# One-hot rows of the gate products, laid out with the places innermost, on one Trainium2 core

## The chip, the cores and the metric

The kernel runs on one core of a Trainium2 chip. That core has four compute engines that each take their own instructions in order: TensorE (PE in the rows; its weight loads are a row kind of their own, PEld), VectorE (DVE), ScalarE (ACT) and GpSimd (POOL), beside SyncE (SP), which here only starts transfers. The metric is the device time of one execution in microseconds (us); of several executions the median is taken.

## The reference, cut to what matters

One layer of a decoder trunk over 1024 prompt tokens and 32 sample tokens: a projection, three token mixers, an output projection, and then a product-key mixture of 16384 single-row experts (PEER). For every token, eight heads choose 16 experts each, so 128 pairs of an expert number and a gate. With `i = 128 a + b` as the expert number, the layer's last part is

```
act  = gelu(x @ peer_u[i])                 # 128 chosen experts of each token
out  = sum over the 128 of  gate * act * peer_v[i]
```

The kernel treats four of the nine token tiles (tiles 2 to 5, 512 tokens, called dense here) without gathering: it computes the scores of all 16384 experts and needs, for each token, a 128 x 128 table of gates `G[a, b]`, which is zero but for the chosen experts. The change is in the code that builds this table.

## The kernel before, in words

**The table of gates.** `g_weights(i, t)` builds it for one dense tile of 128 tokens. Two transposes put the tile's 128 expert numbers and gates on the partitions (partition = place in the list of 128 choices, column = token). From the numbers come `a` and `b` as 16-bit floats in the tile `fx`, and the gate as a 16-bit head and a 16-bit rest. Then, for blocks of `BB = 16` tokens, VectorE writes the tile `ab`, which holds three one-hot arrays: the one for `a` (`ab[:, 0]`), the one for `b` times the head of the gate (`ab[:, 1]`), and the one for `b` times the rest (`ab[:, 2]`, also called `eq`). ScalarE does the last multiplication for the first `NL = 6` tokens of a block. TensorE multiplies, for each token, the transposed `a` rows by the two `b` arrays (two 128 x 128 matmuls into the tile `pgm`, four tokens to a bank). ScalarE copies each bank out to two tiles `gs`, and for each 32 tokens two transfers of 1 MB write these to the DRAM table `G_d`. There are 4 tiles x 8 blocks = 32 blocks and 1024 such matmuls. `ab` has two buffers, each `gs` half has one.

**What runs beside it.** A tile's table can start when the tile is routed (`g_route`, `g_choice`: matmuls `pqr` and top-k work on VectorE). `g_pre` computes the scores of 32 of the 128 expert blocks ahead (matmuls `psd`, line 1070). The other five tiles are done by gathering: POOL starts one indirect transfer for each expert row of 128 tokens (`row`, line 1272); VectorE uses a `peer_u` row (line 1299), TensorE a pair of `peer_v` rows (`acc`, line 1356); six buffers hold such rows. All of these share the engines in one program order. When the last table is written the kernel closes its front tiles and goes on to the dense part (`psd` and `po` matmuls), which lasts to the end.

**The order of the work** is set by generators with declared costs and by a scheduler that orders each engine's instructions by a modelled timeline.

Of the kernel before, what the change touches and what calls it, by code (L numbers as in the profile page):

```python
# [8 lines left out]
F16 = mybir.dt.float16  # L9
# [4 lines left out]
AF = mybir.ActivationFunctionType  # L14
ALU = mybir.AluOpType
AX = mybir.AxisListType

P = 128
# [36 lines left out]
BB = 16  # L55
NL = 6
PRE = [4 * g + 3 for g in range(32)]
GROUP = 4
SW, SU, SV, SG_, SC = 2.0 ** 8, 2.0 ** 8, 2.0 ** 6, 2.0 ** 12, 0.25
# [18 lines left out]
def kernel(ctx: ExitStack, tc: tile.TileContext, A, O):  # L78
    nc = tc.nc
    mm, tr = nc.tensor.matmul, nc.tensor.transpose  # L80
    V, S = nc.vector, nc.scalar
# [72 lines left out]
    def bank(name, shape=(P, 512)):  # L154
        return psum.tile(list(shape), F32, name=name, tag="f", bufs=5)

    def keep(name, shape, dtype=F32, bufs=1):
        return small.tile(list(shape), dtype, name=name, tag=name, bufs=bufs)
# [123 lines left out]
    C = {}  # L282
# [707 lines left out]
    scale = keep("scale", [P, 4])  # L990
# [28 lines left out]
    def g_weights(i, t):  # L1019

        sc = cur["build"]
        if "rep" not in C:
            C["rep"] = sc.tile("rep", [P, P, BB], F16)
            V.tensor_copy(C["rep"], iota16.unsqueeze(2).to_broadcast([P, P, BB]))
        IF, G = (top[t][2][:, e].rearrange("p h j -> p (h j)") for e in range(2))
        pt = bank("ptg", (P, 2, P))
        tr(pt[:, 0, :], IF, ident)
        tr(pt[:, 1, :], G, ident)
        ix = sc.tile("ix", [P, 2, P], I32)
        V.tensor_copy(ix[:, 0, :], pt[:, 0, :])  # L1030
        V.tensor_scalar(ix[:, 1, :], ix[:, 0, :], P - 1, None, op0=ALU.bitwise_and)
        V.tensor_scalar(ix[:, 0, :], ix[:, 0, :], 7, None, op0=ALU.arith_shift_right)
        fx = sc.tile("fx", [P, 4, P], F16, 2)
        fl = sc.tile("fl", [P, P], F32, 2)
        V.tensor_copy(fx[:, 0:2, :], ix)
        V.tensor_scalar(fx[:, 2, :], pt[:, 1, :], SG_, None, op0=ALU.mult)
        V.scalar_tensor_tensor(out=fx[:, 3, :], in0=pt[:, 1, :], scalar=SG_, in1=fx[:, 2, :], op0=ALU.mult,
                               op1=ALU.subtract)
        V.tensor_copy(fl, fx[:, 3, :])
        yield 0.4, 1.0, 0  # L1040
        for b in range(P // BB):
            ab = sc.tile("ab", [P, 3, P, BB], F16, 2)
            f = [fx[:, j, b * BB:b * BB + BB].unsqueeze(1).to_broadcast([P, P, BB]) for j in range(4)]
            eq = ab[:, 2]
            V.tensor_tensor(out=ab[:, 0], in0=C["rep"], in1=f[0], op=ALU.is_equal)
            V.tensor_tensor(out=eq, in0=C["rep"], in1=f[1], op=ALU.is_equal)
            V.tensor_tensor(out=ab[:, 1], in0=eq, in1=f[2], op=ALU.mult)  # L1047
            V.tensor_tensor(out=eq[:, :, NL:], in0=eq[:, :, NL:], in1=f[3][:, :, NL:], op=ALU.mult)
            for j in range(NL):
                S.activation(eq[:, :, j], eq[:, :, j], AF.Copy, scale=fl[:, b * BB + j:b * BB + j + 1])  # L1050
            if b * BB % TB == 0:
                gs = [sc.tile("gs", [P, 64, TB], F32, 2) for _ in range(2)]
            for t4 in range(0, BB, 4):
                pg = bank("pgm", (P, 4, P))
                for j in range(4):
                    for e in range(2):
                        mm(pg[:, j, :], lhsT=ab[:, 0, :, t4 + j], rhs=ab[:, 1 + e, :, t4 + j], start=(e == 0), stop=(e == 1))  # L1057
                t0 = b * BB % TB + t4
                for e in range(2):
                    S.activation(gs[e][:, :, t0:t0 + 4].rearrange("p c t -> p t c"), pg[:, :, 64 * e:64 * e + 64], AF.Copy)  # L1060
                yield 0.6, 1.1, 0.4 * MB
            if (b + 1) * BB % TB == 0:
                for e in range(2):
                    nc.sync.dma_start(G_d[i * (P // TB) + b * BB // TB, :, 64 * e:64 * e + 64, :], gs[e])
# [197 lines left out]
    iota16 = keep("iota16", [P, P], F16)  # L1262
# [264 lines left out]
    def g_gates():  # L1527
        yield from wait("build")
        for i, t in enumerate(DENSE):
            yield from wait(("routed", t))  # L1530
            yield from g_weights(i, t)
            ready.add(("weights", t))
# [208 lines left out]
```

## Time and profile before

| | |
|---|---|
| median of three runs | 3297.21 us (3287.35 to 3303.12) |
| the profiled execution, own time | 3293.14 us |
| its span, first to last instruction | 3291.4 us |
| TensorE busy / VectorE / ScalarE / GpSimd, share of the span | 87% / 67% / 31% / 40% |
| mean transfer rate | 297 GB/s |

The busy share of TensorE is an average over stages with other limits. The tables are built from about 1080 us to 1710 us of the span; what happens there is read from that stretch.

### The profile page before, as it was taken

To read this page: it belongs to the slowest core of one execution; us is meant where nothing else is said; L and a number is where in the kernel's file an instruction comes from. 1 tells how busy PE (TensorE), PEld (TensorE's weight loads), DVE (VectorE), ACT (ScalarE), POOL (GpSimd) and SP (SyncE) were. 2 spreads that over 40 slices of the span, in tenths; PEclk is the share of its full clock that TensorE was granted. 3 is DMA by queue.
4 is the path that set the end of the run, shared out by engine and by line. 5 is a ranking of instruction groups with operands and counts; after the bars stand their busy time and mean duration, and the time that the engine had idled before them with its cause. 6 is when DMAs were issued, how large, how long until landed. Compare 5 with 4: busy or idle time off the path is not lost.

```text
span 3291.4 us, 45024 instructions
## 1 busy us (share of the span) xinstructions
PE 2878.7 (87%) x16366; PEld 1477.0 (45%) x16366; DVE 2206.4 (67%) x5761; ACT 1019.0 (31%) x1654; POOL 1323.3 (40%) x1096
## 2 busy tenths in 40 slices
PE   6878993587976899997788699999999999999996
PEld 3447942334654566444342464433444443333331
DVE  2443998777788877655445678766777776555546
ACT  3413243111021444456561124232323322222220
POOL 0000366545444533432233410544555554455544
PEclk8988996688978899996559799999999999999997
DMA  8743898889898888777578864999999999999986
GB/s 296 249 172 134 293 350 297 294 308 325 317 345 304 298 292 302 261 286 274 206 257 310 311 209 156 343 331 328 364 354 356 352 354 346 344 353 354 351 314 208
DMA packets 376498, 979.03 MB, mean 297 GB/s; under 512 B 37477, under 2 KB 116452, under 8 KB 372172
## 3 DMA queue, kind: packets, MB, share of 16 engines
q0 software_dynamic: 156672, 570.49, 47.8%
q1 hardware_dynamic: 219604, 405.67, 35.5%
q8 instruction: 128, 2.10, 0.3%
q14 instruction: 94, 0.77, 0.1%
HBM read 907.07 MB, written 69.02 MB: 297 GB/s over the span
## 4 chain that ended last, share of the span: by engine, by line
PE 57%; DMA 11%; DVE 6%; issue 4%; ACT 2%; POOL 1%; SPq 0%; POOLq 0%; DVEq 0%; ACTq 0%
PE psd L1070 17%; PE po L1177 16%; PE acc L1356 7%; PE pgm L1057 6%; DMA row<-in_peer_v,iT 6%; PE pqr L880 5%; DMA row<-in_peer_u,ii 3%; PE py L809 2%; POOL row L1272 1%; DVE row L1299 1%; ACT ab L1050 1%; DMA wo<-in_w_o 1%; PE ps L890 1%; DMA e<-x_d 1%; PE pvp L279 1%
## 5 line engine op out<-in xcount | busy, mean ns | idle before, releaser
L1272 POOL DMA_INDIRECT row<-in_peer_u,ii x544 | 672.4, 1236 | 1036.4 <-DVE ii L1295 316.0
L1272 POOL DMA_INDIRECT row<-in_peer_v,iT x544 | 647.6, 1190 | 875.0 <-PE acc L1356 494.8
L1299 DVE SCALAR_TENSOR_TENSOR row<-row,x2u 128x1024 f32<-128x1024 f32 x544 | 660.2, 1217 | 304.0 <-DMA row<-in_peer_u,ii 288.1
L1070 PE MATMUL psd<-xd,us 128*128 128x512 f16 x3072 | 709.5, 381 | 18.7 <-DMA xd<-xd_d 8.3
L1177 PE MATMUL po<-vs,coef 128*128 128x512 f16 x3072 | 701.3, 379 | 3.0 <-ACT coef L1167 1.7
L1070 PEld LDWEIGHTS <-us 128*128 128x128 f16 x3072 | 295.8, 99 | 430.9 <-issue 79.8
L1177 PEld LDWEIGHTS <-coef 128*128 128x128 f16 x3072 | 291.0, 98 | 430.3 <-issue 89.0
L1356 PE MATMUL acc<-row,cexp 128*32 128x512 f32 x2176 | 330.7, 662 | 127.4 <-DMA row<-in_peer_v,iT 127.1
L1057 PE MATMUL pgm<-ab 128*128 128x128 f16 x1024 | 265.4, 419 | 43.6 <-DVE ab L1047 23.1
L880 PE MATMUL pqr<-x2T,wpq 128*128 128x128 f32 (+1 forms) x2304 | 286.0, 283 | 1.9 <-DVE ns_s L707 0.7
L880 PEld LDWEIGHTS pqr<-x2T,wpq 128*128 128x128 f32 x2304 | 280.9, 199 | 10.9 <-DVE CT_s L712 1.5
L1160 ACT ACTIVATE act<-psd,scale 128x512 f32<-128x512 f32 x96 | 65.8, 685 | 513.5 <-PE psd L1070 503.7
L1057 PEld LDWEIGHTS <-ab 128*128 128x128 f16 x1024 | 149.7, 148 | 154.0 <-issue 40.4
L1186 DVE SCALAR_TENSOR_TENSOR acc<-po,scale,acc 128x512 f32<-128x512 f32 x248 | 182.9, 744 | 45.7 <-PE po L1177 40.4
L1162 DVE SCALAR_TENSOR_TENSOR act<-act,scale,g 128x512 f32<-128x512 f32 x128 | 95.7, 748 | 151.6 <-ACT act L1160 128.1
L1140 ACT ACTIVATE vs<-v 128x1024 f16<-128x1024 f32 x128 | 135.5, 1062 | 144.2 <-PE po L1177 123.0
L1060 ACT ACTIVATE gs<-pgm 128x256 f32<-128x256 f32 x256 | 139.8, 672 | 103.7 <-PE pgm L1057 96.8
L1141 DVE SCALAR_TENSOR_TENSOR vs<-v,vs 128x1024 f16<-128x1024 f32 x128 | 155.8, 1217 | 20.6 <-ACT vs L1140 19.7
L1356 PEld LDWEIGHTS acc<-row,cexp 128*32 128x32 f32 x2176 | 47.8, 112 | 259.3 <-DMA row<-in_peer_v,iT 148.3
L809 PE MATMUL py<-wo,Y 128*128 128x512 f32 (+1 forms) x288 | 141.2, 635 | 19.1 <-DMA wo<-in_w_o 10.6
L1050 ACT ACTIVATE ab<-ab,fl 128x128 f16<-128x128 f16 x192 | 118.8, 1034 | 84.5 <-DVE ab L1047 84.5
L279 PEld LDWEIGHTS <-w 128*128 128x128 f16 x2160 | 124.0, 100 | 26.4 <-issue 23.1
(346 smaller groups left out, 2923.2 us busy)
## 6 DMA issues: line engine op xcount, KB each, us to landing
v<-in_peer_v SPq DMA_DIRECT2D x128, 512.0 KB
u<-in_peer_uT SPq DMA_DIRECT2D x96, 512.0 KB
wpq<-in_w_pq SPq DMA_DIRECT2D x80, 512.0 KB
G_d<-gs SPq DMA_DIRECT2D x32, 1024.0 KB
g<-G_d SPq DMA_DIRECT2D x32, 1024.0 KB
wada<-in_w_ada SPq DMA_DIRECT2D x48, 512.0 KB
wf<-in_w_in SPq DMA_DIRECT2D x44, 512.0 KB
wo<-in_w_o SPq DMA_DIRECT2D x40, 512.0 KB
```

The source lines that it names most:

```text
L279: mm(out, lhsT=x if cs is None else y, rhs=y if cs is None else x, start=(i + k == 0), stop=(i == len(ps) - 1 and k == KD - 1))
L809: mm(py[t, e][:ns[t]], lhsT=Y_[t][:, k + j, :ns[t]], rhs=w[:, j, :], start=(k + j == 0), stop=(k + j == KD - 1))
L880: mm(pq[:, i, :ns[t]], lhsT=w[:, k, :], rhs=X2[t][:, k, :ns[t]], start=(k == 0), stop=(k == KD - 1))
L1050: S.activation(eq[:, :, j], eq[:, :, j], AF.Copy, scale=fl[:, b * BB + j:b * BB + j + 1])
L1057: mm(pg[:, j, :], lhsT=ab[:, 0, :, t4 + j], rhs=ab[:, 1 + e, :, t4 + j], start=(e == 0), stop=(e == 1))
L1070: mm(ps, lhsT=us[a][:, k, :], rhs=xd[:, :, b, k, :], start=(m == 0), stop=(m == 23))
L1141: V.scalar_tensor_tensor(out=vs[:, 1], in0=v, scalar=SV, in1=vs[:, 0], op0=ALU.mult, op1=ALU.subtract)
L1177: mm(po, lhsT=d[:, a, i * P:(i + 1) * P], rhs=vs[:, b, c % 2, :], start=(m == 0), stop=(m == 3 * GROUP - 1))
L1186: V.scalar_tensor_tensor(out=a, in0=po, scalar=scale[:, 3:4], in1=a, op0=ALU.mult, op1=ALU.add)
L1272: nc.gpsimd.indirect_dma_start(out=s[:], out_offset=None, in_=A[table], in_offset=bass.IndirectOffsetOnAxis(ap=idx, axis=0))
L1299: V.scalar_tensor_tensor(out=s, in0=s, scalar=1.0, in1=x2, op0=ALU.mult, op1=ALU.mult, accum_out=sv[:, k:k + 1])
L1356: return mm(pv[e][g:g + 32, :], lhsT=l, rhs=s[:, e * 512:e * 512 + 512], start=(j == 0), stop=(j == nj - 1), skip_group_check=True)
```

## The change

Before, the innermost run of `ab` is the 16 tokens of a block, so one token's 128 places lie 16 elements (32 bytes) apart. After, the tile is `[3, tokens, places]`: one token's 128 places lie side by side. The comparison runs over tokens, then places; the value of a token is the same for all 128 places, and so that it can be read as a run of two adjacent 16-bit values, each value stands twice in `fx` and is read 64 times over as a pair. The tile of repeated place numbers (`rep`) is gone; `iota16`, 128 numbers, is read for each token instead.

```
--- before.py
+++ after.py
@@ def g_weights(i, t):
         sc = cur["build"]
-        if "rep" not in C:
-            C["rep"] = sc.tile("rep", [P, P, BB], F16)
-            V.tensor_copy(C["rep"], iota16.unsqueeze(2).to_broadcast([P, P, BB]))
...
-        fx = sc.tile("fx", [P, 4, P], F16, 2)
+
+        fx = sc.tile("fx", [P, 4, P, 2], F16, 2)
         fl = sc.tile("fl", [P, P], F32, 2)
-        V.tensor_copy(fx[:, 0:2, :], ix)
-        V.tensor_scalar(fx[:, 2, :], pt[:, 1, :], SG_, None, op0=ALU.mult)
-        V.scalar_tensor_tensor(out=fx[:, 3, :], in0=pt[:, 1, :], scalar=SG_, in1=fx[:, 2, :], op0=ALU.mult,
-                               op1=ALU.subtract)
-        V.tensor_copy(fl, fx[:, 3, :])
+        twice = lambda a: a.unsqueeze(2).to_broadcast([P, P, 2])
+        for e in range(2):
+            V.tensor_copy(fx[:, e], twice(ix[:, e, :]))
+        V.tensor_scalar(fx[:, 2], twice(pt[:, 1, :]), SG_, None, op0=ALU.mult)
+        V.scalar_tensor_tensor(out=fl, in0=pt[:, 1, :], scalar=SG_, in1=fx[:, 2, :, 0], op0=ALU.mult, op1=ALU.subtract)
+        V.tensor_copy(fx[:, 3], twice(fl))
         yield 0.4, 1.0, 0
         for b in range(P // BB):
-            ab = sc.tile("ab", [P, 3, P, BB], F16, 2)
-            f = [fx[:, j, b * BB:b * BB + BB].unsqueeze(1).to_broadcast([P, P, BB]) for j in range(4)]
+            ab = sc.tile("ab", [P, 3, BB, P], F16, 2)
+            pairs = lambda a: a.rearrange("p t (c e) -> p t c e", e=2)
+            f = [fx[:, j, b * BB:b * BB + BB, :].unsqueeze(2).to_broadcast([P, BB, P // 2, 2]) for j in range(4)]
+            one = iota16.rearrange("p (c e) -> p c e", e=2).unsqueeze(1).to_broadcast([P, BB, P // 2, 2])
             eq = ab[:, 2]
-            V.tensor_tensor(out=ab[:, 0], in0=C["rep"], in1=f[0], op=ALU.is_equal)
-            V.tensor_tensor(out=eq, in0=C["rep"], in1=f[1], op=ALU.is_equal)
-            V.tensor_tensor(out=ab[:, 1], in0=eq, in1=f[2], op=ALU.mult)
-            V.tensor_tensor(out=eq[:, :, NL:], in0=eq[:, :, NL:], in1=f[3][:, :, NL:], op=ALU.mult)
+            V.tensor_tensor(out=pairs(ab[:, 0]), in0=one, in1=f[0], op=ALU.is_equal)
+            V.tensor_tensor(out=pairs(eq), in0=one, in1=f[1], op=ALU.is_equal)
+            V.tensor_tensor(out=pairs(ab[:, 1]), in0=pairs(eq), in1=f[2], op=ALU.mult)
+            V.tensor_tensor(out=pairs(eq[:, NL:]), in0=pairs(eq[:, NL:]), in1=f[3][:, NL:], op=ALU.mult)
             for j in range(NL):
-                S.activation(eq[:, :, j], eq[:, :, j], AF.Copy, scale=fl[:, b * BB + j:b * BB + j + 1])
+                S.activation(eq[:, j], eq[:, j], AF.Copy, scale=fl[:, b * BB + j:b * BB + j + 1])
...
-                        mm(pg[:, j, :], lhsT=ab[:, 0, :, t4 + j], rhs=ab[:, 1 + e, :, t4 + j], start=(e == 0), stop=(e == 1))
+                        mm(pg[:, j, :], lhsT=ab[:, 0, t4 + j, :], rhs=ab[:, 1 + e, t4 + j, :], start=(e == 0), stop=(e == 1))
```

Every line below `g_weights` has moved down by one. The number of instructions is the same on each engine, but for three more on VectorE; GpSimd's order is unchanged. From the first table on, the scheduler has ordered some of the rest a little otherwise.

VectorE, in the last of the four tables, two blocks of 16 tokens (`row` is a gathered expert row that VectorE multiplies by its token). Before:

```order
L1045 TENSOR_TENSOR ab<-rep,fx 128x2048
L1046 TENSOR_TENSOR ab<-rep,fx 128x2048
L1045 TENSOR_TENSOR ab<-rep,fx 128x2048
L1046 TENSOR_TENSOR ab<-rep,fx 128x2048
L1299 SCALAR_TENSOR_TENSOR row,sv<-row,x2u 128x1024
L1047 TENSOR_TENSOR ab<-ab,fx 128x2048
L1299 SCALAR_TENSOR_TENSOR row,sv<-row,x2u 128x1024
L1047 TENSOR_TENSOR ab<-ab,fx 128x2048
L1299 SCALAR_TENSOR_TENSOR row,sv<-row,x2u 128x1024
L1048 TENSOR_TENSOR ab<-ab,fx 128x128x10 x2
```

The same place after the change:

```order
L1046 TENSOR_TENSOR ab<-iota_106,fx 128x2048
L1047 TENSOR_TENSOR ab<-iota_106,fx 128x2048
L1300 SCALAR_TENSOR_TENSOR row,sv<-row,x2u 128x1024 x2
L1048 TENSOR_TENSOR ab<-ab,fx 128x2048
L1046 TENSOR_TENSOR ab<-iota_106,fx 128x2048
L1047 TENSOR_TENSOR ab<-iota_106,fx 128x2048
L1049 TENSOR_TENSOR ab<-ab,fx 128x1280
L1048 TENSOR_TENSOR ab<-ab,fx 128x2048
L1300 SCALAR_TENSOR_TENSOR row,sv<-row,x2u 128x1024
L1049 TENSOR_TENSOR ab<-ab,fx 128x1280
```

Before, the first block's third step stands behind the second block's two comparisons; after, it stands ahead of them.

ScalarE, at the end of the last table (`ab` is the multiplication of six tokens, `gs` the copies out of the banks). Before:

```order
L1050 ACTIVATE ab<-ab,fl 128x128 x6
L1060 ACTIVATE gs<-pgm 128x4x64
L1050 ACTIVATE ab<-ab,fl 128x128 x6
L1060 ACTIVATE gs<-pgm 128x4x64 x15
L1050 ACTIVATE ab<-ab,fl 128x128 x6
```

After:

```order
L1061 ACTIVATE gs<-pgm 128x4x64 x5
L1051 ACTIVATE ab<-ab,fl 128x128 x6
L1061 ACTIVATE gs<-pgm 128x4x64 x11
L1051 ACTIVATE ab<-ab,fl 128x128 x6
L1061 ACTIVATE gs<-pgm 128x4x64 x16
```

The second block's six multiplications now stand behind five copies of the first block instead of one.

## Rows read from the trace of the kernel before

**Rows 1.** The page's slices of the span (40 of 82.3 us each): TensorE's busy tenths, the TensorE clock that was granted in tenths of full speed, and the busy share of the transfer engines in tenths.

```profile
PE   6878993587976899997788699999999999999996
PEclk8988996688978899996559799999999999999997
DMA  8743898889898888777578864999999999999986
```

**Rows 2.** Busy time by stretch. Columns: stretch, its length, then busy us (and instructions) of PE, PEld, DVE, ACT and POOL, the granted clock as a share of 2.4 GHz, the busy share of the transfer engines, GB/s.

```profile
1080.00:1200.00 120.00, 114.37 (x713) 76.79 (x714) 92.66 (x320) 51.18 (x92) 53.47 (x40) 0.93 0.83 294
1200.00:1460.00 260.00, 249.51 (x1354) 137.69 (x1353) 175.01 (x598) 127.20 (x218) 101.69 (x76) 1.00 0.80 284
1460.00:1710.00 250.00, 204.45 (x826) 105.85 (x825) 129.32 (x166) 157.95 (x283) 72.15 (x59) 0.59 0.66 238
800.00:1000.00 200.00, 174.32 (x1113) 117.79 (x1114) 153.24 (x586) 29.31 (x70) 96.01 (x82) 0.88 0.93 334
2300.00:2800.00 500.00, 497.50 (x2448) 204.43 (x2446) 380.06 (x545) 151.37 (x188) 262.17 (x221) 1.00 0.97 353
```

**Rows 3.** From the chain that ended last, in order of time: start, length, what.

```profile
1332.77 1.85 PE acc L1356 x16
1366.23 8.23 DMA row<-in_peer_v,iT
...
1405.01 9.85 DMA row<-in_peer_v,iT
...
1540.72 1.86 PE acc L1356 x8
...
1587.07 13.58 PE pgm L1057 x56
```

**Rows 4.** The same stretches, the gate matmuls of line 1057 alone: busy us (and number) of PE and PEld, then the clock, the transfers' share and GB/s.

```profile
1080.00:1200.00 120.00, 21.88 (x81) 11.70 (x81) 0.93 0.83 294
1200.00:1460.00 260.00, 82.91 (x312) 45.50 (x313) 1.00 0.80 284
1460.00:1710.00 250.00, 160.59 (x632) 92.53 (x631) 0.59 0.66 238
```

**Rows 5.** Groups of instructions by shape, of the whole span: line, engine, operation, out<-in, shapes and number | busy us of the group, mean ns of one | idle time before.

```profile
L1057 PE MATMUL pgm<-ab 128*128 128x128 f16 x1024 | 265.4, 419 | 43.6 <-DVE ab L1047 23.1 <-ACT gs L1060 17.7 <-ACT ab L1050 2.6
L279 PE MATMUL pj<-X,w 128*128 128x128 f16 x1536 | 97.2, 224 | 4.4 <-ACT gates L339 3.2 <-issue 1.2
L1070 PE MATMUL psd<-xd,us 128*128 128x512 f16 x3072 | 709.5, 381 | 18.7 <-DMA xd<-xd_d 8.3 <-ACT us L1087 8.3 <-DVE us L1088 2.1
L1046 DVE TENSOR_TENSOR ab<-rep,fx 128x2048 f16<-128x2048 f16 x32 | 38.9, 1217 | 0.0
L1048 DVE TENSOR_TENSOR ab<-ab,fx 128x1280 f16<-128x1280 f16 x32 | 26.1, 829 | 0.1
L974 DVE TENSOR_TENSOR WK<-PF,rank 128x1024 f16<-128x1024 f16 x16 | 11.0, 686 | 2.1 <-PE pqr L880 1.1 <-DVE PF L973 0.5 <-PE ps L890 0.5
L1299 DVE SCALAR_TENSOR_TENSOR row<-row,x2u 128x1024 f32<-128x1024 f32 x544 | 660.2, 1217 | 304.0 <-DMA row<-in_peer_u,ii 288.1 <-issue 6.0 <-DMA row<-in_peer_v,iT 4.2
L1035 DVE CAST fx<-ix 128x256 f16<-128x256 int32 x4 | 1.1, 282 | 0.0
L1024 DVE COPY rep<-iota 128x2048 f16<-128x2048 f16 x1 | 1.2, 1215 | 0.0
```

**Rows 6.** Bursts in order of time: start, length, engine, line, what and how many. The first two are TensorE's other 128-column matmuls with both operands side by side in memory, at the full and at the half clock; the third is ScalarE's multiplication of 128 elements that lie side by side, with two operands of one value per partition; the fourth is the one of the gate tables.

```profile
90.71 5.48 PE L279 MATMUL pj<-X,w 128*128 128x128 f16 x95
278.90 2.23 PE L279 MATMUL pj<-X,w 128*128 128x128 f16 x19
68.96 3.19 ACT L327 ACTIVATE X<-X,adaT 128x128 f32<-128x128 f32 x8 [3.44 <-DMA X<-in_xT]
1687.66 3.81 ACT L1050 ACTIVATE ab<-ab,fl 128x128 f16<-128x128 f16 x6 [2.57 <-DVE ab L1047]
```

**Rows 7.** One round of 64 gate matmuls (32 tokens) near the end of the last table, merged rows of all engines: start, length, engine, line, what, and in brackets the idle time before it and what ended it.

```profile
1662.16 1.94 PE L1356 MATMUL acc<-row,cexp 128*32 128x512 f32 x8
1667.02 3.13 PE L1057 MATMUL pgm<-ab 128*128 128x128 f16 x11 [2.92 <-DVE ab L1047]
1672.06 11.92 PE L1057 MATMUL pgm<-ab 128*128 128x128 f16 x48 [0.24 <-ACT ab L1050]
1683.91 1.94 PE L1356 MATMUL acc<-row,cexp 128*32 128x512 f32 x8
...
1662.32 1.22 DVE L1045 TENSOR_TENSOR ab<-rep,fx 128x2048 f16<-128x2048 f16 x1 [3.40 <-ACT gs L1060]
...
1674.30 3.70 ACT L1060 ACTIVATE gs<-pgm 128x256 f32<-128x256 f32 x7
...
1664.36 1.13 POOL L1272 DMA_INDIRECT row<-in_peer_v,iT  x1 [13.45 <-PE acc L1356]
```

**Rows 8.** Waits between 1460 and 1710 us: who waited <- for whom: us in total, times, longest.

```profile
POOL row L1272 <- PE acc L1356: 122.3, 11, 17.5
...
DVE ab L1045 <- PE pgm L1057: 35.4, 8, 7.1
...
PE pgm L1057 <- DVE ab L1047: 23.1, 6, 8.0
PE pgm L1057 <- ACT gs L1060: 17.7, 5, 7.7
```

## The prediction

> **What bounds the kernel now.** I read the slices first. TensorE is busy nearly everywhere, but slices 13 to 20 of the page, where the tables are built, are not its best: the clock drops to half in two of them and the transfers fall to 6 tenths [rows 1]. The table by stretch cuts this in two. From 1080 to 1460 us TensorE is the limit: 114.4 + 249.5 = 364 of 380 us busy. From 1460 to 1710 us nothing is full: TensorE 204 of 250, ScalarE 158, VectorE 129, transfers 0.66 [rows 2]. After 2300 us both TensorE (497.5 of 500) and the transfers (0.97) are full [rows 2]; the change touches nothing there.
>
> The second view is the chain of waits in order of time. It runs over TensorE almost without a break, and the pieces of line 1057 are long (13.58 us for 56) [rows 3]. Two pieces are waits for a gathered row of about 8 to 10 us [rows 3]; keep them in mind as what could be late next. So TensorE's time at line 1057 is time of the kernel, in a stage that is not yet at the limit of its transfers.
>
> **What a gate matmul costs, before and after.** The 1024 take 265.4 us, 0.26 each [rows 5]. They take that at the full clock (82.9 / 312 = 0.27) and at the half clock (160.6 / 632 = 0.25) alike [rows 4]: not the array sets their pace but the reading of operands whose elements lie 32 bytes apart. The nearest rows with operands side by side are the 128-column matmuls of line 279, each too with a weight load of its own: 5.48 / 95 = 0.058 us at the full clock, 2.23 / 19 = 0.117 at the half clock [rows 6], 97.2 / 1536 = 0.063 over all [rows 5]. I take 0.058 where the clock is full and 0.117 where it is half.
>
> A page would make this dearer: the Trainium skill, "TensorE: Matmul & The Clock Gate", section "Back-to-back issue gap", gives about 81 ns per matmul for a stream of weight load and 128 columns. By it the 393 of the first stretch would take 32 us instead of 23, an estimate from that page; line 279 is measured here, so the row decides.
>
> **First stretch, 1080 to 1460 us.** 81 + 312 = 393 gate matmuls take 104.8 us [rows 4]; at 0.058 they take 23, so 82 us of TensorE come free. Not all can be cashed. The transfers were busy 0.83 x 120 + 0.80 x 260 = 308 us; at the fullest share that I see, 0.97, they need 317 us, so the stretch can lose at most 63 [rows 2]. VectorE needs 268 us there [rows 2], no limit. The row waits of 8 to 10 us show that parts are already paced by gathers, where a faster TensorE only waits longer [rows 3]. I take 40, about half of what comes free and midway between 63 and 15; 15 is a fifth of the 82, if row waits pace most of the stretch once TensorE is quicker.
>
> **Second stretch, 1460 to 1710 us.** 632 matmuls are 9.9 rounds of 64, 25.3 us a round; a clean one lasts 1683.91 - 1662.16 = 21.75 us [rows 7]. In it TensorE ends the round before, VectorE then does the second block's comparisons and the first block's third step (2.92 us of idle TensorE), 16 matmuls follow at the pace of ScalarE's multiplications, and then 48 in 11.92 us [rows 7]. After the change, each engine's need for a round is:
> - TensorE: 64 x 0.117 = 7.5, plus 1.9 for the gathered pair: 9.4 us.
> - ScalarE: 12 multiplications at 3.19 / 8 = 0.40 (at most: that row reads two values per partition, these read one) are 4.8; they took 3.81 / 6 = 0.64 [rows 6]. 16 copies at 3.70 / 7 = 0.53 are 8.5 [rows 7]. Sum 13.3.
> - VectorE: two blocks of 3 x 1.22 + 0.83 = 4.5 are 9.0; three gathered rows at 1.22 make 12.7 [rows 5].
> - Transfers: 0.66 x 250 = 165 us of full work [rows 2], 170 at a share of 0.97, so 17.2 a round.
>
> So the transfers are next. From the round itself: the 48 matmuls shrink from 11.92 to the pace of the copies (12 x 0.53 = 6.4), and the first 16 from 5.0 to about 3: 7.5 less, 25.3 - 7.5 = 17.8. The two ways agree. I take 17.8 x 9.9 = 177 + 1 = 178: **72 us less**; at best 80 (transfers at 0.97). At worst half of the freed time returns as waits, 36. What hides there now is the gather: POOL waits 122 us in 250 for TensorE to use a pair of rows [rows 8]. A sooner use starts the next gather sooner, so that wait shrinks by itself.
>
> **VectorE's price for the pairs.** The three full steps are 1.217 us and the short one 0.829, two elements a cycle [rows 5]. No row has an operand read in runs of two; the nearest is line 974, an operand read in runs of 16, and it keeps that pace (0.686 for 1024) [rows 5]. Lower bound: unchanged. Upper bound: one element a cycle, as line 1299 (1.217 for 1024 [rows 5]): +1.07 for each of three steps and +0.67 for the short one, 3.9 us a block, 124 us in all. I take unchanged, as in line 974.
>
> What would decide is stated in the Trainium skill, "Vector Engine (DVE) Microarchitecture Reference", section 5.1: two a cycle if all operands are 16-bit, with an innermost step of one and more than one element in it. A run of two satisfies it, so by the page too the sum stays; no run here shows it yet.
>
> **Small parts.** A tile's head does one more copy and the 128-wide steps become 256-wide: four tables x about 0.5 us (0.282 for a 256-wide one [rows 5]) = +2; the `rep` copy goes, -1.2 [rows 5]. Together +1. VectorE and ScalarE are reordered as shown under the change; the third step now stands ahead of the second block's comparisons, which wait for TensorE (35.4 us in all [rows 8]). That helps the round, and I have put nothing down for it.
>
> **Sum.** 3293.1 (own time of the profiled run) - 40 - 72 + 1 = 3182. The median of the runs before is 4 us above that run, so the forecast for a median is **3186 us**, 3.4% less.
>
> **Rivals.**
> 1. *The freed time comes back as waits for transfers.* Rows of gathers and the writes of the table set the round, and the first stretch follows its gathers. For it: row waits on the chain already [rows 3]. Against: the transfers run at 0.66 and 0.80 here and at 0.97 elsewhere, where a gather starts every 500 / 221 = 2.3 us [rows 2], against 250 / 59 = 4.2 in the second stretch. Gains of 36 and 15: 3293 - 51 + 1 + 4 = 3247 us.
> 2. *VectorE drops to one element a cycle.* A round of VectorE is then 12.7 + 7.8 = 20.5 us, so the second stretch gains at most (25.3 - 20.5) x 9.9 = 48, less the waits that stay, some 25; the first has 12 blocks more of 3.9 us on top of 268 and gains about 20. 3293 - 45 + 1 + 4 = 3253 us.
> 3. *Slower: the clock.* TensorE with less to do in the first stretch may be granted less. The gathered matmuls take twice as long at half clock (16 in 1.85 us against 8 in 1.86 [rows 3]). The stretch's TensorE work after the change is 364 - 82 = 282 us at full clock. It turns the whole into a loss of over 0.5% when 282 x (1 + s) exceeds 380 + 72 + 16, so when s = 66% of it runs at half clock; at 75% the stretch takes 494 us: 3293 + 114 - 72 + 4 = 3339. Against: from 800 to 1000 us TensorE is busy 87% and granted 0.88; here it would be 282 / 340 = 83%. Only the stretch that is nearly all gate matmuls has 0.50.
> 4. *The layout is not what makes them slow,* and 0.26 stays: 3297. Against: line 279 has the same shape, type and weight loads and is four times faster [rows 6].
>
> **How the numbers follow.** Forecast 0.70 (3186, own range 3150 to 3225), rival 1 0.15, rival 2 0.08, rival 3 0.03, rival 4 0.04. Best end: -63 - 80 + 1 + 4 on 3293 = 3155; I reach 13 lower for the reordering that I left unpriced, 3142. Upper end: rival 2, 3253. What is left out is rivals 3 and 4 and the tails. A measurement of this kernel tells about 0.5% (16 us) from no change: faster covers the forecast and rivals 1 and 2, 0.92 with their tails cut; same 0.05, slower 0.03.
>
> **What would show it.** In the profile of the changed kernel: line 1058 at about 0.06 us each in the first stretch and 0.12 or less in the second, its weight loads shorter than the 92.53 / 631 = 0.147 us of now [rows 4]; lines 1046 to 1048 still at 1.22 us (2.3 is rival 2); line 1051 in bursts of six under 2.6 us; the last gate matmul at about 1600 us, and everything after it shifted as a whole, with the same 0.97 of transfers. Transfers in the second stretch at 0.9 or more say that they are the next limit; TensorE waiting for rows at 0.7 says rival 1; a granted clock under 0.7 between 1080 and 1400 us says rival 3. I am wrong if the round does not fall under 20 us though each engine needs less than 18, because the order of the work strings their needs in a row; or if what follows the tables waits for something that does not come sooner.

## The result, and the profile after

The changed kernel takes **3192.0 us** (median of four, 3181.4 to 3205.7) where the kernel before took 3295.8 beside it: a ratio of **0.969** (95%: 0.964 to 0.973), 104 us less. The forecast was 3186. Its profiled execution took 3195.2 us, 98 less than that of before.

The page's slices answer [rows 1], counted from 0 as in the prediction; they are 79.8 us each now. The tables end in slice 19. The clock's hole, 5 tenths in slices 19 and 20 before, is 6 tenths in slice 19, with 7 ahead of it and 8 behind. The transfers are at 8 and 9 tenths in slices 13 to 19; before, they fell from 8 to 7 and then 5 (not 6, as the prediction has it).

```profile
PE   5888995387978699885566999999999999999996
PEclk7988997688979799997687999999999999999997
DMA  8754798899898899899898647999999999999986
```

The operations of the tables answer [rows 5]. Columns: busy us of the group, mean ns of one, then the idle time before it.

```profile
L1058 PE MATMUL pgm<-ab 128*128 128x128 f16 x1024 | 98.9, 251 | 64.5 <-DVE ab L1048 30.1 <-ACT gs L1061 21.8 <-ACT ab L1051 11.6
L1051 ACT ACTIVATE ab<-ab,fl 128x128 f16<-128x128 f16 x192 | 59.3, 391 | 86.7 <-DVE ab L1048 86.7
L1046 DVE TENSOR_TENSOR ab<-iota,fx 128x2048 f16<-128x2048 f16 x32 | 38.7, 1218 | 15.6 <-PE pgm L1058 11.9 <-ACT gs L1061 3.7
L1049 DVE TENSOR_TENSOR ab<-ab,fx 128x1280 f16<-128x1280 f16 x32 | 26.1, 817 | 0.1
```

The gate matmuls fell from 265.4 to 98.9 us; VectorE's steps, with every value now read as a pair, stayed at 1.218 and 0.817. By stretch (columns as in [rows 2]; the second cut is where the third table starts, the third behind the last gate matmul):

```profile
1080.00:1200.00 120.00, 108.59 (x772) 76.00 (x773) 95.54 (x331) 46.20 (x98) 49.32 (x41) 0.94 0.90 325
1200.00:1450.00 250.00, 219.65 (x1504) 120.38 (x1503) 193.62 (x618) 127.57 (x258) 114.54 (x87) 0.97 0.90 330
1450.00:1590.00 140.00, 69.99 (x604) 48.88 (x602) 110.14 (x143) 92.42 (x232) 65.58 (x47) 0.68 0.90 331
2300.00:2800.00 500.00, 492.43 (x2443) 197.91 (x2441) 354.49 (x510) 145.30 (x182) 257.58 (x214) 1.00 0.95 343
```

No compute engine is full in the third row (VectorE leads with 110 of 140 us), while the transfers run at 0.90 from 1080 us to the end of the tables.

**Where the 98 us are.** Three events mark the way, and their rows follow, of before and then of after (start, length, what): the transposes at the head of the third table (`ptg`), the last gate matmuls, and the first matmul of the front tiles' output projection (`py`), which waits for its weights `wo`.

```profile
1512.62 0.39 PE L1027 MATMUL ptg<-ident,rt 128*128 128x128 f32 x1
...
1699.62 4.98 PE L1057 MATMUL pgm<-ab 128*128 128x128 f16 x20
...
1732.82 6.11 PE L809 MATMUL py<-wo,Y 128*128 128x512 f32 x8 [5.15 <-DMA wo<-in_w_o]
```

```profile
1450.66 0.42 PE L1024 MATMUL ptg<-ident,rt 128*128 128x128 f32 x1
...
1587.66 2.72 PE L1058 MATMUL pgm<-ab 128*128 128x128 f16 x24 [1.11 <-ACT gs L1061]
...
1625.58 6.20 PE L809 MATMUL py<-wo,Y 128*128 128x512 f32 x8 [18.82 <-DMA wo<-in_w_o]
```

The first two tables end 62 us sooner. The last two take 139.4 us instead of 191.6, so the last gate matmul starts 114 us sooner (1590.1, was 1704.2). Then 7 are lost before `py`, and 9 behind it: from `py` to the end are 3193.5 - 1625.6 = 1567.9 us, 1558.6 before. These are single executions; by the medians the kernel gained 104 us, so 10 of the 114 did not reach the end, not 16.

### The profile page after: what moved, and what is told of

It is laid out like the page before. It is cut to its first block, busy times and chain, and to the rows that moved or that the text cites. A ratio compares the mean times of both kernels' runs of the same rounds, so it can differ in the third digit from the quotient of the medians.

```text
span 3193.5 us, 45027 instructions
## 1 busy us (share of the span) xinstructions
PE 2726.1 (85%) x16366; PEld 1405.0 (44%) x16366; DVE 2205.3 (69%) x5764; ACT 952.3 (30%) x1654; POOL 1312.7 (41%) x1096
## 4 chain that ended last, share of the span: by engine, by line
PE 49%; DMA 14%; issue 6%; DVE 5%; POOL 3%; ACT 2%; SPq 0%; POOLq 0%; DVEq 0%; ACTq 0%
PE po L1178 16%; PE psd L1071 16%; PE acc L1357 7%; DMA row<-in_peer_v,iT 7%; PE pqr L880 4%; DMA row<-in_peer_u,ii 4%; POOL row L1273 3%; PE py L809 2%; DVE row L1300 1%; DMA G_d<-gs 1%; ACT gs L1061 1%; PE pgm L1058 1%; DMA wo<-in_w_o 1%; PE pvp L279 1%; PE ps L890 1%
## 5 line engine op out<-in xcount | busy, mean ns | idle before, releaser
L1058 PE MATMUL pgm<-ab 128*128 128x128 f16 x1024 | 98.9, 251 | 64.5 <-DVE ab L1048 30.1
L1061 ACT ACTIVATE gs<-pgm 128x256 f32<-128x256 f32 x256 | 125.9, 641 | 49.8 <-PE pgm L1058 33.0
L279 PEld LDWEIGHTS <-w 128*128 128x128 f16 x2160 | 124.2, 100 | 23.7 <-issue 20.6
L1168 ACT ACTIVATE coef<-act 128x512 f16<-128x512 f32 x128 | 80.1, 626 | 153.7 <-DVE act L1163 153.3
L1125 DVE SCALAR_TENSOR_TENSOR us<-u,us 128x1024 f16<-128x1024 f32 x96 | 117.0, 1220 | 11.6 <-ACT us L1124 11.4
```

The costliest lines, as they stand in the source:

```text
L279: mm(out, lhsT=x if cs is None else y, rhs=y if cs is None else x, start=(i + k == 0), stop=(i == len(ps) - 1 and k == KD - 1))
```

## The experiments

Ratios are to the kernel before, run beside each group on the same chip; its medians were 3296.0, 3300.8 and 3296.7 us there.

**The two stretches apart.** The first kernel uses the new layout for the first two tables and the old one for the last two; the second the reverse. (To hold both, `fx` has one buffer, and its line numbers lie 27 higher.)

```diff
+        layout = "nnn" if i < 2 else "ooo"      # second kernel: "ooo" if i < 2 else "nnn"
...
+            ab = sc.tile("ab", [P, 3, BB * P], F16, 2)
+            arr = [ab[:, k].rearrange("p (t c) -> p t c", t=BB) if layout[k] == "n" else
+                   ab[:, k].rearrange("p (c t) -> p t c", t=BB) for k in range(3)]
...
+                        mm(pg[:, j, :], lhsT=arr[0][:, t4 + j], rhs=arr[1 + e][:, t4 + j], start=(e == 0), stop=(e == 1))
```

> The new layout for the first two of the four tables, the old one for the last two. These two tables hold the 393 gate matmuls of the first stretch and 119 of the second. If my terms hold (40 us for the first stretch, 72 for the second), this kernel gains 40 + 72 x 119 / 632 = 54 us: about 3242 us. Rival: while TensorE is shared with other work the gathers pace the first stretch, so nothing is gained there and all of it comes from the last two tables: about 3280 us.

Measured: 3238.0 us, ratio 0.983 (0.980 to 0.987), 58 us less.

> The old layout for the first two tables, the new one for the last two, which hold 512 of the 632 gate matmuls of the second stretch. By my terms 72 x 512 / 632 = 58 us are gained: about 3238 us. By the rival (gathers pace the first stretch) nearly the whole gain, about 95 us: 3200 us. The gains of this kernel and of the first-two kernel should add up to that of the whole change (104 us) if the two stretches do not give anything back to each other.

Measured: 3264.3 us, 0.992 (0.990 to 0.994), 32 us less. The terms of the sum, shared out by tables, were 40 + 72 x 119 / 632 = 54 for the first two and 58 for the last two, so the first came as expected and the second at little more than half. The marks tell why a total is not the tables' own gain. In the first kernel the third table starts at 1441.1, 72 us sooner than before where the terms gave 54, and `py` at 1656.1, 77 sooner, of which 59 reach the end of the profiled execution. In the second the last two tables take 145 us instead of 191.6, a gain of 46 where the terms gave 58, `py` comes 42 sooner and the profiled execution, the fastest of its four, ends 40 sooner. So the 58 of the first kernel agree with the term by two misses that cancel, and of the 26 that the second falls short, 12 lie in its tables. Together the two gain 90 us of the whole change's 104; the intervals do not part these two numbers.

**Which operand is slow.** Two kernels keep the old layout in one operand: `layout = "onn"` (the stationary one, `a`) and `layout = "noo"` (the two moving ones, and ScalarE's).

> Only the stationary operand (the one-hot array of a) is kept in the old layout, 32 bytes from element to element; both moving operands and ScalarE's six multiplications are in the new one. If the moving operand's reading sets the pace of 0.25 us, the gate matmuls take about 0.1 us or little more (weight loads 148 ns instead of 98 may show up as 0.15) and the kernel is near 3192 to 3205 us. If the weight load sets it, they stay at 0.25 us and the kernel is near 3290 us less what ScalarE gives (some 10 us).

Measured: 3202.6 us, 0.973 (0.971 to 0.975).

> The mirror: the stationary operand in the new layout, both moving operands and ScalarE's multiplications in the old one. If the moving operand sets the pace: 0.25 us a matmul although weight loads take 98 ns, ScalarE's multiplication at 1.05 us, kernel near 3290 us. If the weight load did: 0.1 us a matmul and the kernel near 3205 us.

Measured: 3306.4 us (seven runs), 1.004 (1.002 to 1.005). The matmuls and weight loads of the two, stationary operand old and then moving operands old:

```profile
L1085 PE MATMUL pgm<-ab 128*128 128x128 f16 x1024 | 104.6, 259 | 69.5 <-ACT gs L1088 35.0 <-DVE ab L1075 30.7 <-ACT ab L1078 3.5
L1085 PEld LDWEIGHTS <-ab 128*128 128x128 f16 x1024 | 94.5, 154 | 99.1 <-issue 53.1 <-DVE ab L1075 36.3 <-DVE row L1327 0.3
```

```profile
L1085 PE MATMUL pgm<-ab 128*128 128x128 f16 x1024 | 256.5, 409 | 45.2 <-DVE ab L1075 23.5 <-ACT gs L1088 18.6 <-ACT ab L1078 3.0
L1085 PEld LDWEIGHTS <-ab 128*128 128x128 f16 x1024 | 120.1, 118 | 175.9 <-issue 45.9 <-DVE ab L1075 30.6
L1078 ACT ACTIVATE ab<-ab,fl 128x128 f16<-128x128 f16 x192 | 116.2, 1021 | 95.1 <-DVE ab L1075 95.1
```

With the moving operand 32 bytes apart a gate matmul costs 256.5 / 1024 = 0.25 us again and all of the gain is gone; with the stationary one so, it costs 0.10 and nearly all of the gain stays. A stationary operand of that kind lengthens its weight load (median 150 ns instead of 98).

The second kernel leaves two rivals little room. Its ScalarE is slow too, but TensorE waits only 3.0 us in all for those multiplications. And in its last table it has the new order on VectorE, with the third step ahead of the next block's comparisons:

```profile
1675.04 1.22 DVE L1075 TENSOR_TENSOR ab<-ab,fs 128x2048 f16<-128x2048 f16 x1
1676.42 1.23 DVE L1073 TENSOR_TENSOR ab<-iota,fx 128x2048 f16<-128x2048 f16 x1 [0.17 <-PE pgm L1085]
```

So the order gains nothing while the moving operand is slow; what it gives beside the new layout no run shows.

**What the pairs are worth.** The new layout, but each value stands once and is read 128 times over:

```diff
-        fx = sc.tile("fx", [P, 4, P, 2], F16, 2)
+        fx = sc.tile("fx", [P, 4, P], F16, 2)
...
-            pairs = lambda a: a.rearrange("p t (c e) -> p t c e", e=2)
-            f = [fx[:, j, b * BB:b * BB + BB, :].unsqueeze(2).to_broadcast([P, BB, P // 2, 2]) for j in range(4)]
-            one = iota16.rearrange("p (c e) -> p c e", e=2).unsqueeze(1).to_broadcast([P, BB, P // 2, 2])
+            pairs = lambda a: a
+            f = [fx[:, j, b * BB:b * BB + BB].unsqueeze(2).to_broadcast([P, BB, P]) for j in range(4)]
+            one = iota16.unsqueeze(1).to_broadcast([P, BB, P])
```

> The new layout without the pairs: each value stands once and is read 128 times over as a run of one. If VectorE keeps two elements a cycle only when the innermost step is one, its full steps go from 1.22 to about 2.28 us and the short one from 0.82 to about 1.5 (3.9 us a block, 124 us of VectorE in all), and the kernel loses some 50 to 60 us of the gain: about 3245 us (my second rival, now made on purpose). If a value that is read again and again costs nothing, the steps stay at 1.22 us and the kernel at 3192 us.

Measured: 3360.2 us, 1.016 (1.013 to 1.020): 168 us over the changed kernel by the medians, 157 by the ratios, and slower than the kernel before. VectorE's steps first, then the waits between 1450 and 1733.6 us, where its last table ends (columns as in [rows 8]):

```profile
L1044 DVE TENSOR_TENSOR ab<-iota,fx 128x2048 f16<-128x2048 f16 x32 | 73.1, 2284 | 8.4 <-PE pgm L1056 6.2 <-ACT gs L1059 2.2
L1047 DVE TENSOR_TENSOR ab<-ab,fx 128x1280 f16<-128x1280 f16 x32 | 47.3, 1483 | 0.1
```

```profile
ACT ab L1049 <- DVE ab L1046: 100.7, 15, 20.0
PE acc L1355 <- DMA row<-in_peer_v,iT: 99.8, 15, 15.2
...
PE pgm L1056 <- DVE ab L1046: 53.5, 9, 14.2
```

The steps take 2.284 and 1.483 us, to 0.01 us the upper bound that the prediction worked out (1.22 + 1.07, 0.83 + 0.67). In the profiled executions the 124 us that VectorE has more to do cost 143 by the last table's end and some 25 behind it: TensorE waits for the tables (53.5 us) and, more, for gathered rows (99.8 us). The Trainium skill, "Vector Engine (DVE) Microarchitecture Reference", section 5.1, asks for an innermost run of more than one element with step one; the two kernels differ in how the token's value is read, as a pair or as one element, and their steps agree with it.

**What else sets the round.** Three kernels change one or two sizes of the changed kernel: blocks of 8 tokens with four buffers, ScalarE's share of a block at 12 tokens, and at none.

```diff
-BB = 16
-NL = 6
+BB = 8            # first kernel, with ab in 4 buffers
+NL = 3            # first kernel; second: NL = 12; third: NL = 0 (BB stays 16 in both)
```

> Blocks of 8 tokens instead of 16, 3 tokens of each for ScalarE, four buffers of half the size: the same memory and the same share of ScalarE. In the changed kernel TensorE waits longest for VectorE's third step. If what is left of a round is this chain through two buffers (VectorE, ScalarE, TensorE, copies), finer blocks shorten it and the kernel is 10 to 25 us faster, about 3175 us, though VectorE's steps cost 10 to 15 us more in all (0.68 for half of 1.22). If transfers or gathered rows hold the round, it stays at 3192 us or loses the 10 us.

Measured: 3201.2 us, 0.970 (0.967 to 0.974).

> ScalarE multiplies 12 tokens of each 16 instead of 6; VectorE's short step then covers 4 tokens instead of 10 (about 0.4 us less a block, 12 us in all), ScalarE has 32 x 6 x 0.3 = 58 us more. If VectorE is what the rounds wait for, 5 to 10 us faster (3185 us). If ScalarE's chain holds the first matmuls of a block, slower by up to 20 us (3210 us). If transfers hold, the same.

Measured: 3210.7 us, 0.970 (0.965 to 0.975).

> ScalarE multiplies none: VectorE's fourth step covers all 16 tokens (1.22 instead of 0.82 us, 13 us more in all), ScalarE has 192 operations less (about 60 us). If the wait for ScalarE's multiplications and its queue hold the round, 5 to 20 us faster (3175 to 3187 us); if VectorE does, slower by up to 10 us.

Measured: 3199.1 us, 0.968 (0.965 to 0.971). None of the three can be told from the changed kernel (0.969, and 0.967 when it was run again, below). So neither the block's size nor ScalarE's share is shown to set the end. Inside the tables twelve may cost something: in the profiled execution, the slowest of its four, the last gate matmul starts at 1628.7, against 1594.1 with none and 1590.1 with six.

**More bytes.** Eight copies of 1 MB from DRAM to DRAM, written behind the writes of the last two tables:

```diff
...
+                if i >= 2:
+                    r = (i - 2) * (P // TB) + b * BB // TB
+                    nc.sync.dma_start(spare_d[r], A["peer_v"][256 * r:256 * r + 256, :])
```

> The changed kernel with 8 more transfers of 1 MB, DRAM to DRAM, one behind each pair of table writes of the last two tables; nothing reads what they write, so only their use of the transfer engines counts. In the changed kernel these engines are busy 0.90 of the time from 1450 to 1590 us at 331 GB/s; 8 MB are 24 us at that rate. If transfers hold the rounds now, the last two tables take 20 to 25 us longer and the kernel is near 3214 us. If the order of the work on VectorE and TensorE holds them, the bytes fit into what is idle: under 8 us, 3195 to 3200 us.

Measured: 3201.5 us, 0.972 (0.969 to 0.974), and its trace says why this decides nothing (columns: durations of one issue, first and last start):

```profile
L1069 SPq DMA_DIRECT2D spare_d<-in_peer_v x8: 488/580/1512, 60.8 to 69.6; - x8
```

The copies wait for nothing, and the scheduler put all eight at the start of the program, 1.4 ms ahead of the stretch that they were meant to load. Whether the transfers limit the tables now stays untested.

**More buffers for the copied tables.** `gs` in four buffers instead of two, paid for with blocks of 8 and one buffer of `fx`; its control has the blocks and the single `fx` but two buffers of `gs`; the third is the changed kernel itself.

```diff
-BB = 16
-NL = 6
+BB = 8
+NL = 3
...
-        fx = sc.tile("fx", [P, 4, P, 2], F16, 2)
+        fx = sc.tile("fx", [P, 4, P, 2], F16)
...
-                gs = [sc.tile("gs", [P, 64, TB], F32, 2) for _ in range(2)]
+                gs = [sc.tile("gs", [P, 64, TB], F32, 4) for _ in range(2)]   # control: 2
```

> Blocks of 8 tokens in two buffers, and with the memory that this frees, the tiles that hold the copies out of the banks in two sets instead of one: ScalarE no longer waits for the write of the last 32 tokens (11.6 us of its waits from 1451 to 1590 us, and 18 us of TensorE's behind it). If this wait holds the rounds, 10 to 20 us faster than its control with one set and about 3180 us; if transfers do, no different from the control.

Measured: 3184.6 us, 0.966 (0.963 to 0.969).

> The control for the second set: blocks of 8 tokens in two buffers (half the memory), one set of copy tiles. With less memory ahead it should be no faster than the changed kernel: 3195 to 3215 us.

Measured: 3192.0 us, 0.970 (0.966 to 0.973).

> The changed kernel itself once more, so that the three others are compared on one chip: 3192 us, between 3180 and 3206.

Measured: 3191.2 us, 0.967 (0.964 to 0.971). The totals hardly differ, but the tables do. Last gate matmuls, in this order (durations of one; first and last start):

```profile
L1058 PE MATMUL pgm<-ab x1024: 216/219/314, 1091.8 to 1565.9; 128*128 128x128 f16 x171
```

```profile
L1058 PE MATMUL pgm<-ab x1024: 216/219/315, 1098.4 to 1607.2; 128*128 128x128 f16 x171
```

```profile
L1058 PE MATMUL pgm<-ab x1024: 216/219/314, 1094.0 to 1585.7; 128*128 128x128 f16 x171
```

Between the first two lie 41 us at the tables' end and 7 at the kernel's end (medians), which their intervals do not part; 10 to 20 had been expected. The control, expected at 3195 or more, is no slower than the changed kernel. More room for the copied tables brings the tables forward (in one execution of each kernel); that the kernel ends sooner by it is not shown. Part of the gain is work put off: behind the first `py` of the front tiles GpSimd still has 601 instructions and TensorE 7506 matmuls, against 588 and 7482 in the control.

**What lies behind the tables**, in the profiled executions of all kernels:

| kernel | last gate matmul | first `py` behind it | `py` to the end |
|---|---|---|---|
| one value, no pairs | 1733.6 | 1769.1 | 1591.9 |
| old layout in the moving operands | 1706.1 | 1736.2 | 1568.5 |
| before | 1704.2 | 1732.8 | 1558.6 |
| new layout in the last two tables | 1654.5 | 1691.0 | 1560.8 |
| twelve tokens on ScalarE | 1628.7 | 1663.3 | 1557.9 |
| new layout in the first two | 1622.9 | 1656.1 | 1576.6 |
| blocks of 8, `gs` in two (control) | 1607.2 | 1639.5 | 1550.5 |
| old layout in the stationary operand | 1597.5 | 1630.2 | 1566.2 |
| no token on ScalarE | 1594.1 | 1627.8 | 1569.4 |
| blocks of 8, `ab` in four | 1593.2 | 1628.9 | 1571.4 |
| after | 1590.1 | 1625.6 | 1567.9 |
| more bytes | 1590.0 | 1626.9 | 1563.1 |
| after, again | 1585.7 | 1621.8 | 1567.8 |
| blocks of 8, `gs` in four | 1565.9 | 1601.5 | 1583.7 |

The rest does not follow the tables' end. It lasts longest behind the latest tables (1591.9 us), and it lasts 1568.5 us in the kernel with the old moving operands, whose tables end like those of before. From the last gate matmul to `py` it is 28.6 us before and 30 to 37 in every other kernel. Part of what is lost before `py` the chain of after shows, in order of time (start, length, what), behind the last gate matmuls:

```profile
1586.99 4.58 ACT gs L1061 x10
1591.58 7.92 DMA G_d<-gs
1599.59 9.31 DMA g<-G_d
...
1616.06 9.32 DMA wo<-in_w_o
1625.58 6.20 PE py L809 x8
```

The same place before:

```profile
1692.63 11.98 PE pgm L1057 x48
1704.61 11.54 PE psd L1070 x48
1719.13 13.48 DMA wo<-in_w_o
1732.82 6.11 PE py L809 x8
```

The weights `wo` stand on SyncE's queue behind the last write of the table and behind the first read of it. Before, they were issued 15 us after the last gate matmul; after, 26 us, because the chain now runs through the table's way to DRAM and back. That is the wait for `wo`, 18.8 us instead of 5.2. No run moved that transfer, so this is read from the chain and not tested.

## Why the prediction was right

**The sum of 112 against 114 measured at the last gate matmul: in part luck.** The first two tables gained 8 us more than the terms, the last two 6 less, and the two misses cancel.

**A gate matmul at 0.058 and 0.117 us: right in kind, the first too low, the second too high.** Between 1200 and 1450 us, at a clock of 0.97, the 417 took 35.78 us, 0.086 each, and 0.105 in the last two tables at 0.68:

```profile
1200.00:1450.00 250.00, 35.78 (x417) 29.21 (x418) 0.97 0.90 330
1450.00:1590.00 140.00, 54.82 (x520) 46.38 (x518) 0.68 0.90 331
```

The second price was for half the clock, and that stretch had more. The line 279 that I took the prices from runs 95 in a row [rows 6]; these come in shorter pieces. One of 32 took 1.95 us, 0.061 each; one of 7 took 1.09, 0.156:

```profile
1439.65 1.95 PE L1058 MATMUL pgm<-ab 128*128 128x128 f16 x32
...
1443.31 1.09 PE L1058 MATMUL pgm<-ab 128*128 128x128 f16 x7 [0.26 <-ACT ab L1051]
```

The piece of 7 goes at the pace of ScalarE's multiplications, six in 1.86 us with two matmuls to each. They are not the whole reason: with no token on ScalarE the mean between 1200 and 1450 us is still 31.31 / 385 = 0.081 us. What the rest is stays open. The 81 ns of the Trainium skill ("TensorE: Matmul & The Clock Gate", "Back-to-back issue gap") are the better mean here and too dear for a long piece. The 0.028 us too little came to some 11 us over the 393 of the first stretch; it did not reach the sum, which had cashed only 40 of the 82 us that came free.

**"Not the array sets their pace but the reading of operands": shown, and sharper than I put it.** It is the moving operand; the stationary one was nearly free. Rival 4 is out.

**First stretch, 40: too small.** By tables the first two gained 62 where the terms gave 54. The transfers went from 0.83 and 0.80 to 0.90 there, as the sum allowed, and TensorE's clock was 0.94 and 0.97, where it had been 0.93 and 1.00. Rival 3's loss of clock did not come.

**Second stretch, 72: right by the round, its make-up only in part.** Forecast 17.8 us a round of 64; the last two tables took 139.4 / 8 = 17.4. In share of the tables that is 52 gained where the terms gave 58, because the rounds there had taken 23.95 before and not the 25.3 of the whole stretch. (The sum itself is 2 us off: 17.8 x 9.9 is 176, and the 1 for small parts is in it twice.) The pieces between two gathered pairs, with 85 gate matmuls in 17.9 us:

```profile
1490.79 1.06 PE L1357 MATMUL acc<-row,cexp 128*32 128x512 f32 x8
1491.79 1.35 PE L1058 MATMUL pgm<-ab 128*128 128x128 f16 x21
1494.92 0.23 PE L1058 MATMUL pgm<-ab 128*128 128x128 f16 x1 [1.79 <-DVE ab L1048]
1495.41 1.09 PE L1058 MATMUL pgm<-ab 128*128 128x128 f16 x7 [0.26 <-ACT ab L1051]
1503.56 5.22 PE L1058 MATMUL pgm<-ab 128*128 128x128 f16 x56 [7.06 <-ACT gs L1061]
1508.71 1.07 PE L1357 MATMUL acc<-row,cexp 128*32 128x512 f32 x8
```

The 48 in 11.92 us of [rows 7] have become 56 in 5.22, and TensorE now waits 7.06 us ahead of them for ScalarE's copies, which themselves waited in part for a `gs` buffer still being written out. The forecast had the 48 follow the copies at 6.4 us and no such wait. The waits between 1451 and 1590 us, against [rows 8]:

```profile
POOL row L1273 <- DVE row L1300: 38.1, 9, 10.2
...
PE pgm L1058 <- DVE ab L1048: 26.2, 6, 8.9
POOL row L1273 <- PE acc L1357: 24.6, 8, 8.5
...
PE pgm L1058 <- ACT gs L1061: 18.1, 7, 7.1
...
ACT gs L1061 <- DMA G_d<-gs: 11.6, 4, 5.3
```

GpSimd's wait for TensorE to use a pair of rows shrank from 122.3 us in 250 to 24.6 in 139, as forecast; its largest is now the one for VectorE to use a row (38.1). TensorE's wait for VectorE's third step did not shrink (23.1 us in 250, 26.2 in 139), though that step now stands ahead of the next comparisons; the help that I named there and left unpriced does not show. The transfers stand at 0.90, the share that I had named as the mark of the next limit. The mark is there, but the run that should have put weight on it missed, so that they *are* the limit is argued. Four `gs` buffers brought the tables' end 20 us further forward at the same share (328 GB/s at 0.89), so the round also hung on that wait, which I had not listed. Its last two tables took 124.2 us (1441.7 to 1565.9), 15.5 a round, less than the 17.2 that I had worked out as the transfers' need: that need was no floor, for gathers can be put off behind the tables.

**VectorE unchanged: right**, 1.218 us. **Rival 2, its opposite, was right in the step and wrong in the price.** I put 3253 on one element a cycle; it measured 3360. The step that failed is "the second stretch gains at most 48, less the waits that stay" and 20 for the first: it let VectorE's longer work lie beside the rest of the round. The run shows it in a row with it: ScalarE waits 100.7 us for VectorE's third step, TensorE 53.5, and the gathers, whose rows VectorE must use in between, come late for another 99.8. With that price the rival should have stood on the slower side, and the upper end of my range did not hold it.

**ScalarE's multiplication at most 0.40 us: right**, 0.391 (six in 1.84 to 1.86 us, where I had said under 2.6). What it bought by itself is not shown: with none or twelve of them the kernel's time cannot be told from that with six.

**"Everything after it shifted as a whole": wrong.** The last gate matmul came 114 us sooner, at 1590 where I had said about 1600, but the end came 98 sooner. I had noted the case as one that would make me wrong and put no number on it. Of the 16 given back, 7 are the wait for `wo`, shown on the chain. Of the 9 behind `py`, 7.7 are busy time of TensorE (1482.4 to 1490.1 us of its tail), 5.8 of them in the matmuls of gathered rows:

```profile
L1356 PE MATMUL acc<-row,cexp 128*32 128x512 f32 x1488 | 215.2, 631 | 55.6 <-DMA row<-in_peer_v,iT 55.3
```

```profile
L1357 PE MATMUL acc<-row,cexp 128*32 128x512 f32 x1480 | 221.0, 632 | 56.6 <-DMA row<-in_peer_v,iT 52.9 <-DVE vy L359 3.7
```

Eight fewer took 5.8 us more; the changed kernel run again has the same tail to 0.1 us and 220.7 us in them. Why they are dearer stays open, and so does whether the 9 us belong to the change: executions of the changed kernel differ by up to 24 us, and with the old moving operands the rest lasts 9.9 us longer than before though TensorE is busy in it for 1481.9 us, as before.

## What to carry to other kernels

Look at how a matmul's moving operand lies in memory before the clock or the array is blamed: a mean far above that of the same shape elsewhere in the trace, the same at both clock levels, was the sign. When an operand must be laid out anew, price what writes it: here the value standing twice was worth some 160 us, more than the whole change gained. And where a stage is shortened, follow the transfers queued behind its last write; what the next stage waits for may be issued there.

## What the runs showed of the hardware

- A 128-column matmul of 16-bit data whose moving elements lie 32 bytes apart took 0.27 us in a stretch at a clock of 1.00 and 0.25 in one at 0.59 [rows 4], four times the 0.061 of adjacent ones in a long piece. The Trainium skill, "SBUF — State Buffer", section "Door 1: The DMA port swizzle", says that reads which each touch another 16-byte line pay a penalty; this agrees. The same spacing in the stationary operand cost 52 ns more a weight load; the matmuls took 104.6 us in all against 98.9, which is within what kernels with adjacent operands show (94.1 to 106.2).
- ScalarE pays for that spacing too: 128 elements took 1055 ns (median) at 32 bytes apart and 387 side by side.
- VectorE keeps its 16-bit pace when a value is re-read as a pair 64 times over (1.218 us for 2048 elements and 0.817 for 1280, so 0.52 ns for each further element), and falls to half of it when the value is re-read singly 128 times (2.284 and 1.483, so 1.04 ns).
